# Stick-breaking attention: the sums over later key blocks as one running sum

## The chip, the cores and the metric

The kernel runs on one core of one Trainium2 chip. The metric is the device time of one execution in microseconds (us). Before the change three runs took 2278.54, 2282.21 and 2282.85 us; their median is 2282.21 us. All else is read from one profiled execution.

## The reference

The kernel computes a chain of layers for 512 positions of width 1024: a state-space layer with a feed-forward layer, a stick-breaking attention layer with a feed-forward layer, a softmax attention layer and a long-convolution layer. The change touches the stick-breaking attention alone. It has 16 heads of width 64, four query blocks and four key blocks of 128:

```python
z = jnp.einsum('bhqd,bhkd->bhqk', qb, kb).astype(jnp.float32)
...
causal = s_idx < t_idx
log_beta = jax.nn.log_sigmoid(z)
log_one_minus = jnp.where(causal, log_beta - z, 0.0)
rem = lax.cumsum(log_one_minus, axis=3, reverse=True) - log_one_minus
w = jnp.where(causal, jnp.exp(log_beta + rem), 0.0)
outs.append(jnp.einsum('bhqk,bhkd->bhqd', w.astype(vb.dtype), vb))
```

With sp(z) = log(1 + exp(z)) = -(log_beta - z), the exponent of a weight is z minus the sum of sp over the key itself and all later causal keys. So each key needs the sum of sp over the later keys of its own block, and over every later block.

## The kernel before, in words

Keys lie on the partitions and queries along the free dimension. `attn` (line 869) first makes the values V, then goes through eight pairs of heads, `b` = 0 to 7. For every second pair it loads and splits a weight tile for k and one for q (`weight`, line 169: the upper part `wh` on ScalarE, the remainder `wl` on VectorE, 128x256 at a time, line 185). For each pair it projects k and q (`proj`, 24 matmuls of 512 columns each), scales them into `kq`, and splits them into `kh`, `kl` and `qh`, `ql` (`ready`, `split`, line 159: the upper part by ScalarE, the remainder by VectorE). Then it calls `sb_heads` (line 940).

All matrix products run in fp32r on numbers split into an upper and a lower part. `sb_heads` works through a pair of heads in three units. Unit 0 holds key blocks 3 and 2 (256 queries each, 128x1024 for both heads; query columns before 256 are not causal for them), unit 1 key block 1 (384 queries, 128x768), unit 2 key block 0 (512 queries, 128x1024). Of each unit:

1. TensorE makes the scores z in a double PSUM tile `pair` (line 956), and adds the causal mask as a product (line 960). There are two such tiles, so unit 2 waits for unit 0's to be read.
2. VectorE takes |z| (line 964, "first step" below), ScalarE exp and ln(1 + .), VectorE adds max(z, 0) (line 967): `e` is the softplus sp. `e` has two buffers (`sbe`).
3. ScalarE rounds `e` to its upper part `sph`, VectorE subtracts for the remainder `spl` (lines 970 and 971; in the profile lines 152 and 140, the helpers).
4. TensorE adds the negative sums onto z (line 982): for the unit's own block with the triangular matrix `ntri`, and for every later block with a matrix of minus ones, `nones`, which sums a block's columns. For this the list `done` keeps the sph and spl of all units so far. A block is four matmuls: upper and lower part, two heads.
5. ScalarE takes exp of the whole unit from PSUM: the weights `wt` (line 985).

After unit 2 the weights times V go into `obank` (line 992), and `oraw` keeps the result. After pair 7 the upper and lower parts of `oraw` are the input of `attn_out`.

The order of the work on each engine is set when the program is built: a scheduler interleaves the projections of the next pair with the sums of the present one, and each engine then runs its list in order, waiting where an input is late. GpSimd has no instruction in the eight pairs.

Of the kernel before, what the change touches and what calls it, by code (L numbers as in the profile page):

```python
# [9 lines left out]
F32 = mybir.dt.float32  # L10
F32R = mybir.dt.float32r
# [3 lines left out]
ALU = mybir.AluOpType  # L15
# [3 lines left out]
P = 128  # L19
S = 512  # L20
# [30 lines left out]
class Kern:  # L51
# [817 lines left out]
    def attn(self):  # L869
        nc, a = self.nc, self.a  # L870
        xn = self.h
        wkv, wq = a["kv_w"], a["attn_w_q"][0]
        with self.sbuf("sb") as sp:
# [7 lines left out]
            mask = self.t([P, 3, P], BF16, "mask", 1, sp)  # L881
            self.act(mask, raw, AF.Copy)
            idr = self.t([P, P], BF16, "idr", 1, sp)
            self.act(idr, self.ident, AF.Copy)
            nones = self.t([P, P], F32R, "nones", 1, sp)
# [5 lines left out]
            self.act(ntri, traw, AF.Copy, scale=-1.0)  # L891

            V = sp.tile([P, 4, D], F32, name="V")
            pend = []
# [18 lines left out]
            os = []  # L913
            for b in range(KB):
# [5 lines left out]
                for n, wt, s in (("k", wk, 1.0), ("q", wqq, 0.125)):  # L920
# [4 lines left out]
                    kq += self.ready(t, None, self.hl(sp, n, 2))  # L925
                os.append(self.sb_heads(sp, b, *kq, V, mask, idr, nones, ntri))
            return [self.ready(o, None, self.hl(self.hp, "h", 8)) for o in os]
# [11 lines left out]

    def sb_heads(self, sp, b, kh, kl, qh, ql, V, mask, idr, nones, ntri):  # L940

# [3 lines left out]
        units = (((3, 256, 0), (2, 256, 256)), ((1, 128, 0),), ((0, 0, 0),))  # L945
        done, wts = [], {}
        for u, parts in enumerate(units):
# [19 lines left out]
            self.stt(e, zv, 0.0, e, ALU.max, ALU.add)  # L967
            sh = self.t([P, 2, W], F32R, f"sph{u}", 2 if u == 0 else 1, sp)
            sl = self.t([P, 2, W], F32R, f"spl{u}", 2 if u == 0 else 1, sp)
            self.act(sh, e, AF.Copy)  # L970
            self.tt(sl, e, sh.bitcast(F32), ALU.subtract)
            for p in parts:
                done.append(p + ((sh, sl),))
            for kb, q0, c0 in parts:
                for kk, qq, cc, sps in done:
                    if kk < kb:
                        continue
                    lhs = ntri if kk == kb else nones
                    for t in sps:
                        for h in range(2):  # L980
                            n = S - qq
                            mm(z[:, h, c0 + qq - q0 : c0 + S - q0], lhs, t[:, h, cc : cc + n],  # L982
                               start=False, stop=True, skip_group_check=True)
            wt = self.t([P, 2, W], F32, f"wt{u}", 1, sp)
# [1081 lines left out]
```

## Time and profile before

| what | value |
|---|---|
| median of three runs | 2282.21 us |
| profiled execution, its own time | 2278.72 us |
| its span, first to last instruction | 2277.0 us |
| mean granted TensorE clock | 0.953 |
| TensorE busy | 2111.4 us, 93% |
| VectorE busy | 1487.8 us, 65% |
| ScalarE busy | 987.9 us, 43% |
| GpSimd busy | 532.0 us, 23% |

Busy times are shares of the whole span; the eight head pairs take 839 to 1037 us of it. In the profile PE is TensorE, DVE VectorE, ACT ScalarE and POOL GpSimd. A line is often that of a helper: line 140 is any `tensor_tensor`, 143 any `scalar_tensor_tensor`, 147 and 149 any `tensor_scalar`, 152 any activation, 192 to 194 the three matmuls of a projection step. A row of the timeline with x2 merges two instructions that follow each other.

### The profile page before, as it was taken

The numbers are of one execution on the slowest core, as the hardware profiler recorded it, in microseconds if no ns is written. First come the engines' busy times: TensorE is split into PE (matmuls) and PEld (weight loads), VectorE is DVE, ScalarE is ACT, GpSimd is POOL, SyncE is SP. The second block draws the span as 40 slices with busy tenths as digits, with TensorE's granted clock in tenths as the row PEclk, the third lists the DMA queues.
The fourth block names the chain that finished last, engine by engine and source line by source line (L and its number), as shares of the span: only waits on it lengthen the run. The fifth ranks groups of instructions, "written<-read, shape, count | busy, mean of one in ns | idle before, by whom it ended". The sixth has DMA issues, their size and how long they took to land.

```text
span 2277.0 us, 29820 instructions
## 1 busy us (share of the span) xinstructions
PE 2111.4 (93%) x11732; PEld 1762.2 (77%) x11732; DVE 1487.8 (65%) x2348; ACT 987.9 (43%) x1496; POOL 532.0 (23%) x471
## 2 busy tenths in 40 slices
PE   6689999999999999989999999989999998888897
PEld 5478888788888887767778878888888877777776
DVE  9787864767665546664665675475687753988843
ACT  5555443332233446664442233434587653222232
POOL 4778621000000100001000000322243333324321
PEclk9789899999999999999999999989999998999899
DMA  5222163334432311112233552312000032222221
GB/s 163 69 62 77 64 206 98 125 99 138 157 125 77 109 59 60 50 38 65 93 120 125 160 177 83 102 52 69 27 1 1 20 111 74 77 91 84 65 74 56
DMA packets 194515, 199.36 MB, mean 88 GB/s; under 512 B 15059, under 2 KB 184550, under 8 KB 194311
## 3 DMA queue, kind: packets, MB, share of 16 engines
q1 hardware_dynamic: 179703, 183.11, 25.3%
q10 hardware_dynamic: 14672, 14.35, 2.1%
q8 instruction: 92, 1.51, 0.3%
q14 instruction: 48, 0.39, 0.1%
HBM read 182.75 MB, written 14.68 MB: 87 GB/s over the span
## 4 chain that ended last, share of the span: by engine, by line
PE 68%; DVE 17%; POOL 4%; issue 4%; ACT 4%; DMA 3%; SPq 0%; DVEq 0%; ACTq 0%; POOLq 0%
PE bank L192 16%; PE bank L194 15%; PE bank L193 15%; PE sc L1376 2%; PE pair L982 2%; DVE spt L140 2%; POOL tm L140 2%; DVE X L140 2%; DVE Y L140 2%; DVE wl L140 1%; PE obank L1799 1%; DMA adaraw<-in_ada_w_dram 1%; DMA wraw<-in_ffn_w_up_dram 1%; ACT wh L152 1%; PE sc L1517 1%
## 5 line engine op out<-in xcount | busy, mean ns | idle before, releaser
L192 PE MATMUL bank<-hh,wh 128*128 128x512 f32 x1472 | 592.9, 403 | 13.8 <-DVE v L143 7.5
L194 PE MATMUL bank<-hh,wl 128*128 128x512 f32 x1472 | 589.8, 401 | 13.3 <-DVE wl L140 13.3
L193 PE MATMUL bank<-hl,wh 128*128 128x512 f32 x1472 | 589.4, 400 | 0.5 <-DVE hl L143 0.5
L152 ACT ACTIVATE wh<-wraw 128x1024 fp32r<-128x1024 f32 (+2 forms) x260 | 245.3, 962 | 352.4 <-PE bank L193 195.2
L140 POOL TENSOR_TENSOR sqa<-sqa,sq 128x512 f32<-128x512 f32 x47 | 70.1, 1492 | 1180.6 <-ACT sq L152 1180.6
L194 PEld LDWEIGHTS bank<-hh,wl 128*128 128x128 f32 x1472 | 283.0, 192 | 78.5 <-DVE wl L140 18.0
L192 PEld LDWEIGHTS bank<-hh,wh 128*128 128x128 f32 x1472 | 282.3, 192 | 77.1 <-issue 7.5
L193 PEld LDWEIGHTS bank<-hl,wh 128*128 128x128 f32 x1472 | 282.6, 192 | 61.9 <-DVE hl L143 2.1
L140 DVE TENSOR_TENSOR wl<-wraw,wh 128x1024 fp32r<-128x1024 f32 (+2 forms) x220 | 245.6, 1133 | 109.3 <-ACT wh L152 108.7
L140 POOL TENSOR_TENSOR wl<-wraw,wh 128x1024 fp32r<-128x1024 f32 x40 | 102.8, 2588 | 177.9 <-ACT wh L152 177.8
L192 PE MATMUL bank<-ah,wh 128*128 128x512 f32 x352 | 137.8, 392 | 0.0
L193 PE MATMUL bank<-al,wh 128*128 128x512 f32 x352 | 137.0, 389 | 0.0
L194 PE MATMUL bank<-ah,wl 128*128 128x512 f32 x352 | 136.5, 390 | 0.3 <-DVE wl L140 0.2
L140 DVE TENSOR_TENSOR fg<-bank,rn 128x512 f32<-128x512 f32 x76 | 52.5, 690 | 106.1 <-PE bank L194 105.4
L140 POOL TENSOR_TENSOR sl<-sp,wh 128x768 fp32r<-128x768 f32 x32 | 59.4, 1857 | 107.8 <-ACT wh L152 57.4
L143 DVE SCALAR_TENSOR_TENSOR adaaccx<-adaraw,silc,adaaccx 128x256 f32<-128x256 f32 x168 | 81.0, 482 | 2.2
L194 PEld LDWEIGHTS bank<-ah,wl 128*128 128x128 f32 x352 | 66.1, 188 | 15.3 <-DVE wl L140 1.4
L193 PEld LDWEIGHTS bank<-al,wh 128*128 128x128 f32 x352 | 66.1, 188 | 13.5
L192 PEld LDWEIGHTS bank<-ah,wh 128*128 128x128 f32 x352 | 66.1, 188 | 13.3
L143 DVE SCALAR_TENSOR_TENSOR fy<-fg,prm,fy 128x511 f32<-128x511 f32 x88 | 65.9, 749 | 13.9 <-ACT fy L152 12.7
L140 POOL TENSOR_TENSOR fX<-spt 128x256 f32<-128x256 f32 x64 | 62.8, 1006 | 42.4 <-DVE spt L140 39.4
L1799 PE MATMUL obank<-X,idft 128*128 128x128 f32 x256 | 43.6, 326 | 29.2 <-DVE X L140 26.8
(557 smaller groups left out, 4328.9 us busy)
## 6 DMA issues: line engine op xcount, KB each, us to landing
wraw<-in_ffn_w_up_dram SPq DMA_DIRECT2D x88, 512.0 KB
adaraw<-in_ada_w_dram SPq DMA_DIRECT2D x24, 1024.0 KB
wraw<-in_ffn_w_down_dram SPq DMA_DIRECT2D x48, 384.0 KB
wraw<-in_hy_w_in_dram SPq DMA_DIRECT2D x32, 512.0 KB
wraw<-in_attn_w_in_dram SPq DMA_DIRECT2D x18, 512.0 KB
kspec<-fX SPq DMA_DIRECT2D x16, 512.0 KB
wraw<-in_ssm_w_glu_dram SPq DMA_DIRECT2D x16, 512.0 KB
wraw<-in_kv_w_dram SPq DMA_DIRECT2D x16, 512.0 KB
```

The lines of the kernel that those rows point to most:

```text
L140: (eng or self.nc.vector).tensor_tensor(out=out, in0=a, in1=b, op=op)
L143: self.nc.vector.scalar_tensor_tensor(out=out, in0=a, scalar=s, in1=b, op0=op0, op1=op1)
L152: return self.nc.scalar.activation(out, a, func, bias=bias, scale=scale, **k)
L192: mm(out, wh[k], xh, start=first and k == 0, stop=False)
L193: mm(out, wh[k], xl, start=False, stop=False)
L194: mm(out, wl[k], xh, start=False, stop=last and k == n - 1)
L982: mm(z[:, h, c0 + qq - q0 : c0 + S - q0], lhs, t[:, h, cc : cc + n], start=False, stop=True, skip_group_check=True)
L1376: mm(s, l, m[:, c], start=i == 0 and k % 2 == 0, stop=True, skip_group_check=True)
L1517: mm(s[:, k], ones, rows[u], start=False, stop=True, skip_group_check=True)
L1799: nc.tensor.matmul(ps[:, r * P : r * P + P], self.idft[:, j, r], Q[:, j, r], start=j == 0, stop=j == 1)
```

## The change

A tile `tail` (128 x 2 x 384, zero at the start) holds the sum of the softplus over the later key blocks. After unit 0, GpSimd adds the softplus of blocks 3 and 2 into its columns from 128 on; after unit 1, it adds `tail` onto unit 1's softplus, in place. Either sum is split into an upper part `sprh` (rounded by ScalarE) and a lower part `sprl` (subtracted by GpSimd). Units 1 and 2 then need one product of `nones` with this sum for all later blocks, where they had one for each. Inside unit 0 block 2 still sums block 3's own sph and spl. `sph` and `spl` of unit 0 have one buffer in place of two.

```diff
+            tail = self.t([P, 2, 384], F32, "tail", 1, sp)
+            nc.gpsimd.memset(tail, 0.0)
...
-        done, wts = [], {}
+        wts = {}
...
-            sh = self.t([P, 2, W], F32R, f"sph{u}", 2 if u == 0 else 1, sp)
-            sl = self.t([P, 2, W], F32R, f"spl{u}", 2 if u == 0 else 1, sp)
+            sh = self.t([P, 2, W], F32R, f"sph{u}", 1, sp)
+            sl = self.t([P, 2, W], F32R, f"spl{u}", 1, sp)
             self.act(sh, e, AF.Copy)
             self.tt(sl, e, sh.bitcast(F32), ALU.subtract)
-            for p in parts:
-                done.append(p + ((sh, sl),))
-            for kb, q0, c0 in parts:
-                for kk, qq, cc, sps in done:
-                    if kk < kb:
-                        continue
-                    lhs = ntri if kk == kb else nones
-                    for t in sps:
-                        for h in range(2):
-                            n = S - qq
-                            mm(z[:, h, c0 + qq - q0 : c0 + S - q0], lhs, t[:, h, cc : cc + n],
-                               start=False, stop=True, skip_group_check=True)
+
+            terms = [(q0, q0, c0, c0, (sh, sl), ntri) for _, q0, c0 in parts]
+            if u == 0:
+                terms.append((256, 256, 256, 0, (sh, sl), nones))
+            else:
+                (_, q0, c0), = parts
+                terms.append((q0, q0 + P, c0, q0, rest, nones))
+            for q0, qq, c0, cc, sps, lhs in terms:
+                for t in sps:
+                    for h in range(2):
+                        n = S - qq
+                        mm(z[:, h, c0 + qq - q0 : c0 + S - q0], lhs, t[:, h, cc : cc + n],
+                           start=False, stop=True, skip_group_check=True)
+
+            if u < 2:
+                rest = [self.t([P, 2, 384], F32R, f"spr{i}", 1, sp) for i in "hl"]
+                if u == 0:
+                    x = tail[:, :, P:]
+                    self.tt(x, e[:, :, :256], e[:, :, 256:], ALU.add, nc.gpsimd)
+                    hi, lo = (t[:, :, P:] for t in rest)
+                else:
+                    x = e
+                    self.tt(x, e, tail, ALU.add, nc.gpsimd)
+                    hi, lo = rest
+                self.split(x, hi, lo, nc.gpsimd)
```

The built order moves with it, in the eight pairs alone. Three places of pair 0 follow; the digit in a tile's name (sph0, spl1, wt2) is the unit.

TensorE, the sums of unit 2, before:

```order
L982 MATMUL pair_1164_7144<-sph0_1156_7094,nones_1105_6438 128x256 x2
L982 MATMUL pair_1164_7144<-spl0_1157_7095,nones_1105_6438 128x256 x2
L982 MATMUL pair_1164_7144<-sph0_1156_7094,nones_1105_6438 128x256 x2
L982 MATMUL pair_1164_7144<-spl0_1157_7095,nones_1105_6438 128x256 x2
L982 MATMUL pair_1164_7144<-sph1_1161_7126,nones_1105_6438 128x384 x2
L982 MATMUL pair_1164_7144<-spl1_1162_7127,nones_1105_6438 128x384 x2
L982 MATMUL pair_1164_7144<-sph2_1166_7158,ntri_1106_6440 128x512 x2
```

And now:

```order
L963 MATMUL pair_1184_7253<-mask_1103_6434,idr_1104_6436 128x384
L193 MATMUL bank_1213_7412<-hl_1093_6366,wh_1205_7368 128x512
L986 MATMUL pair_1169_7152<-spl2_1172_7167,ntri_1106_6440 128x512 x2
L986 MATMUL pair_1169_7152<-sprh_1166_7145,nones_1105_6438 128x384 x2
L986 MATMUL pair_1169_7152<-sprl_1167_7146,nones_1105_6438 128x384 x2
L194 MATMUL bank_1213_7412<-hh_1092_6365,wl_1206_7369 128x512
```

The six rows of column sums of units 0 and 1 have become two, of sprh and sprl, and these stand behind the unit's own spl2.

ScalarE, from unit 0's rounding on, before:

```order
L152 ACTIVATE sph0_1156_7094<-sbe_1155_7089 128x1024
L152 ACTIVATE sph1_1161_7126<-sbe_1160_7121 128x768
L152 ACTIVATE kh_1173_7218<-kq_1172_7216 128x512
L152 ACTIVATE wh_1196_7370<-wraw_1198_7372,prm1_882 128x256 x2
L152 ACTIVATE wh_1196_7370<-wraw_1199_7382,prm1_882 128x256 x3
L152 ACTIVATE wt0_1158_7110<-pair_1154_7074 128x1024
L152 ACTIVATE wh_1196_7370<-wraw_1199_7382,prm1_882 128x256
L152 ACTIVATE wt1_1163_7142<-pair_1159_7112 128x768
```

And now:

```order
L152 ACTIVATE sph0_1157_7096<-sbe_1156_7091 128x1024
L152 ACTIVATE sprh_1159_7112<-tail_1108_6444 128x2x256
L152 ACTIVATE sph1_1164_7133<-sbe_1163_7128 128x768
L152 ACTIVATE kh_1178_7218<-kq_1177_7216 128x512
L152 ACTIVATE wh_1205_7368<-wraw_1207_7370,prm1_882 128x256 x2
L152 ACTIVATE wh_1205_7368<-wraw_1208_7380,prm1_882 128x256 x2
L152 ACTIVATE wt0_1161_7117<-pair_1155_7076 128x1024
L152 ACTIVATE sprh_1166_7145<-sbe_1163_7128 128x768
L152 ACTIVATE wt1_1168_7150<-pair_1162_7119 128x768
```

A rounding of the first sum now stands ahead of sph1, and one of the second sum ahead of wt1, and so ahead of all that follows.

VectorE from unit 0's subtraction to unit 2's first step, before:

```order
L140 TENSOR_TENSOR spl0_1157_7095<-sbe_1155_7089,sph0_1156_7094 128x1024
L140 TENSOR_TENSOR spl1_1162_7127<-sbe_1160_7121,sph1_1161_7126 128x768
L140 TENSOR_TENSOR kl_1174_7219<-kq_1172_7216,kh_1173_7218 128x512
L143 SCALAR_TENSOR_TENSOR wl_1197_7371<-wraw_1198_7372,prm1_882,wh_1196_7370 128x256 x4
L143 SCALAR_TENSOR_TENSOR wl_1197_7371<-wraw_1199_7382,prm1_882,wh_1196_7370 128x256 x4
L147 TENSOR_SCALAR sbe_1165_7153<-pair_1164_7144 128x1024
```

And now:

```order
L140 TENSOR_TENSOR spl0_1158_7097<-sbe_1156_7091,sph0_1157_7096 128x1024
L140 TENSOR_TENSOR spl1_1165_7134<-sbe_1163_7128,sph1_1164_7133 128x768
L140 TENSOR_TENSOR kl_1179_7219<-kq_1177_7216,kh_1178_7218 128x512
L143 SCALAR_TENSOR_TENSOR wl_1206_7369<-wraw_1207_7370,prm1_882,wh_1205_7368 128x256 x4
L143 SCALAR_TENSOR_TENSOR wl_1206_7369<-wraw_1208_7380,prm1_882,wh_1205_7368 128x256 x2
L147 TENSOR_SCALAR sbe_1170_7161<-pair_1169_7152 128x1024
L143 SCALAR_TENSOR_TENSOR wl_1206_7369<-wraw_1208_7380,prm1_882,wh_1205_7368 128x256
```

Of the eight weight remainders ahead of the first step six are left, and the other two follow it.

GpSimd, its first instructions in the stage, where nothing stood before:

```order
L894 MEMSET tail_1108_6444 128x768
L140 TENSOR_TENSOR tail_1108_6444<-sbe_1156_7091 128x2x256
L140 TENSOR_TENSOR sprl_1160_7113<-tail_1108_6444,sprh_1159_7112 128x2x256
L140 TENSOR_TENSOR sbe_1163_7128<-sbe_1163_7128,tail_1108_6444 128x2x384
L140 TENSOR_TENSOR sprl_1167_7146<-sbe_1163_7128,sprh_1166_7145 128x768
```

Of these five the last four come back in each pair; in the program they stand between the rows of VectorE above.

## Rows read from the trace of the kernel before

**Rows 1.** Stretches: length, busy PE PEld DVE ACT POOL (count), granted clock, DMA, GB/s.

```profile
839.50:984.50 145.00, 144.02 (x814) 105.42 (x814) 92.95 (x126) 95.84 (x137) 0.00 (x0) 1.00 0.14 44
984.50:1036.60 52.10, 39.50 (x203) 28.42 (x199) 31.00 (x33) 32.39 (x39) 0.00 (x0) 0.84 0.13 41
```

**Rows 2.** List of waits, TensorE, 839 to 985 us: total us, times, longest us.

```profile
PE obank L992 <- ACT wt L152: 1.0, 3, 0.3
```

**Rows 3.** Timeline, TensorE: start us, us, engine, line, op, tile, shapes, count.

```profile
897.73 0.40 PE L982 MATMUL pair<-sph,nones 128*128 128x256 f32 x2
897.96 0.40 PE L982 MATMUL pair<-spl,nones 128*128 128x256 f32 x2
```

**Rows 4.** Chain that ended last, pair 0: start us, us, what.

```profile
853.40 0.29 PE bank L192
...
858.11 0.32 PE pair L956 x2
```

**Rows 5.** Line 140, GpSimd: count, ns min/median/max, first and last start us, forms.

```profile
L140 POOL TENSOR_TENSOR sqa<-sqa,sq x47: 1287/1420/1999, 331.7 to 2259.4; 128x512 f32<-128x512 f32 x47
L140 POOL TENSOR_TENSOR sl<-sp,wh x32: 1814/1833/2577, 1628.0 to 1839.7; 128x768 fp32r<-128x768 f32 x32
```

**Rows 6.** Timeline, GpSimd and VectorE, output projection.

```profile
1061.65 1.93 POOL L140 TENSOR_TENSOR sqa<-sqa,sq 128x512 f32<-128x512 f32 x1 [5.22 <-ACT sq L152]
...
1060.07 2.36 DVE L140 TENSOR_TENSOR wl<-wraw,wh 128x1024 fp32r<-128x1024 f32 x2 [0.17 <-ACT wh L152]
1062.35 1.78 DVE L143 SCALAR_TENSOR_TENSOR hl<-xT,prm,hh 128x512 fp32r<-128x512 f32 x1
```

**Rows 7.** Lines 140 and 143, VectorE, same columns as rows 5.

```profile
L140 DVE TENSOR_TENSOR ff<-bank,fdec x32: 657/692/693, 128.3 to 296.5; 128x512 f32<-128x512 f32 x32
...
L140 DVE TENSOR_TENSOR fab<-fab,fab x16: 676/807/1981, 131.2 to 297.9; 128x512 f32<-128x512 f32 x16
...
L143 DVE SCALAR_TENSOR_TENSOR hl<-xT,prm,hh x16: 748/1404/1791, 320.8 to 1084.7; 128x512 fp32r<-128x512 f32 x16
```

**Rows 8.** Timeline, VectorE, pair 0.

```profile
845.26 2.09 DVE L143 SCALAR_TENSOR_TENSOR sbe<-pair,sbe 128x1024 f32<-128x1024 f32 x2 [1.95 <-ACT sbe L152]
...
847.87 2.09 DVE L140 TENSOR_TENSOR spl<-sbe,sph 128x1024 fp32r<-128x1024 f32 x2
...
850.47 3.25 DVE L143 SCALAR_TENSOR_TENSOR wl<-wraw,prm,wh 128x256 fp32r<-128x256 f32 x8
853.63 1.22 DVE L147 TENSOR_SCALAR sbe<-pair 128x1024 int32<-128x1024 int32 x1
```

**Rows 9.** Timeline, ScalarE, pair 0.

```profile
846.67 1.78 ACT L152 ACTIVATE sph<-sbe 128x1024 fp32r<-128x1024 f32 x2
848.35 0.62 ACT L152 ACTIVATE kh<-kq 128x512 fp32r<-128x512 f32 x1
...
857.27 0.62 ACT L152 ACTIVATE qh<-kq 128x512 fp32r<-128x512 f32 x1
```

**Rows 10.** Timeline, VectorE, pair 3, unit 2: the first step.

```profile
924.51 1.22 DVE L147 TENSOR_SCALAR sbe<-pair 128x1024 int32<-128x1024 int32 x1 [1.57 <-PE pair L960]
```

**Rows 11.** Timeline, VectorE, pair 6, and the first step of pair 7.

```profile
991.78 2.09 DVE L140 TENSOR_TENSOR spl<-sbe,sph 128x1024 fp32r<-128x1024 f32 x2
...
996.90 1.22 DVE L140 TENSOR_TENSOR wl<-wraw,wh 128x1024 fp32r<-128x1024 f32 x1
998.03 1.22 DVE L147 TENSOR_SCALAR sbe<-pair 128x1024 int32<-128x1024 int32 x1
...
1004.97 1.22 DVE L140 TENSOR_TENSOR spl<-sbe,sph 128x1024 fp32r<-128x1024 f32 x1
...
1010.26 1.22 DVE L147 TENSOR_SCALAR sbe<-pair 128x1024 int32<-128x1024 int32 x1 [2.33 <-PE pair L960]
```

**Rows 12.** Stretches as in rows 1, two of 2 us in the second part.

```profile
1000.00:1002.00 2.00, 0.00 (x0) 0.00 (x0) 2.00 (x3) 1.97 (x4) 0.00 (x0) 0.93 0.50 177
1006.00:1008.00 2.00, 2.00 (x9) 1.35 (x9) 1.41 (x2) 0.68 (x1) 0.00 (x0) 0.50 0.79 266
```

More of the change, by code (lines that the diff above doesn't have):

```diff
@@ L925, in attn @@
                     kq += self.ready(t, None, self.hl(sp, n, 2))
-                os.append(self.sb_heads(sp, b, *kq, V, mask, idr, nones, ntri))
+                os.append(self.sb_heads(sp, b, *kq, V, mask, idr, nones, ntri, tail))
             return [self.ready(o, None, self.hl(self.hp, "h", 8)) for o in os]
@@ L938, in attn_out, with sb_heads @@
                 done(m)
-    def sb_heads(self, sp, b, kh, kl, qh, ql, V, mask, idr, nones, ntri):
+    def sb_heads(self, sp, b, kh, kl, qh, ql, V, mask, idr, nones, ntri, tail):
         nc = self.nc
```

## The prediction

> **What bounds the kernel now.** First the stage: the change lies in the attention of the second layer alone, and the table of stretches shows it as 839.5 to 1036.6 us, in two parts [rows 1]. In the first, 145 us, TensorE is busy 144.0 us at full clock while VectorE has 93.0 and ScalarE 95.8; the list of waits gives TensorE 1.0 us of idle time there [rows 2]. So any TensorE work that goes is time, unless something else becomes late. In the second, 52.1 us, the projections that fill TensorE's gaps run out: it is busy 39.5 us at a mean clock of 0.84, and the chain goes through VectorE and ScalarE. GpSimd does nothing in either. Behind the stage the output projection starts at once, so what the stage gains or loses reaches the end in full.
>
> Second, the pace of TensorE. Matmul durations overlap; the cost is the distance between starts. Four 256-column matmuls start in two rows 0.235 us apart: 0.118 us each [rows 3]. A 512-column projection matmul costs 0.235 us: 20 of them stand between the starts 853.40 and 858.11 [rows 4].
>
> **The change part by part.** *Removed.* Per head pair three blocks of column sums, each of four 256-column matmuls: 12, and 96 in eight pairs (320 matmuls of this line become 224). At 0.118 us that is 1.42 us a pair, 11.3 us in all; 8.5 us lie in the first part (pairs 0 to 5), and 2.8 us in the second, where they only count if nothing later takes their place.
>
> *Added on GpSimd.* Per pair an addition and a subtraction on 128x512, and the same on 128x768. The rows give 1.29 us (the least of 47 accumulations) and 1.83 us (the median of 32 subtractions) [rows 5], so 6.2 us a pair, 50 us in all. That is a quarter of the stage: GpSimd doesn't become the bound. The views of 2x256 occur nowhere before; I take the contiguous price, and the median of the accumulation, 1.42 us, as the upper one (0.3 us more a pair). The 128x768 memset of the tail stands ahead of the first pair's addition in a queue that is empty in the stage: nothing; uncovered it would cost less than a 128x768 operation with two inputs, 1.8 us.
>
> *Added on ScalarE.* Two roundings a pair: 0.62 us like kh for 512 columns, some 0.8 for 768 (sph0 and sph1 take 1.78 together) [rows 9]: 11.6 us in 197, onto 128 busy. It fits, but each stands in ScalarE's queue in front of other steps and waits there for GpSimd: the first in front of sph1, the second in front of wt1 and unit 2's exponential.
>
> *Single buffers.* sph0 and spl0 need one buffer, as only their own unit reads them. The two spr tiles are written again at the earliest 1.8 us (one GpSimd addition) after their last reader could start. Nothing.
>
> *What decides: GpSimd and VectorE in each other's way.* The trace has such pairs of operations [rows 6]. GpSimd's 128x512 addition at 1061.65 took 1.93 us, where 1.29 is its least: it waited until VectorE's two subtractions ended at about 1062.4. VectorE's remainder at 1062.35 then took 1.78 us, where 0.75 is its least [rows 7]: it waited until GpSimd was through. So they take turns, each for a whole instruction. Between 130 and 300 us, where GpSimd works most, the product of a PSUM and an SBUF tile (ff) never rose above 0.69 us, and the sum of two SBUF tiles of the same size (fab) reached 1.98 [rows 7]. I read it so: an instruction of VectorE with two SBUF inputs (spl, kl, ql, the weight remainders wl, hl) excludes a GpSimd operation, one that reads PSUM doesn't. The Trainium skill says the same as a rule that speaks against this change (SBUF — State Buffer, section "Who interferes with whom": a VectorE instruction with two SBUF inputs contends with a GpSimd instruction that reads SBUF, and whichever comes second is blocked entirely). By the rule the sum is the one that follows; without it, rival A. The rows bear the rule out.
>
> Now pair 0, by the rows of VectorE and ScalarE [rows 8, 9] and the new order. The first softplus is ready at 846.4. GpSimd adds 846.5 to 847.8 while VectorE reads PSUM. Rounding to 848.5; sph1 moves 0.7 us back, to 849.2. GpSimd's subtraction is due at 848.5, but VectorE is in spl0 until 849.1, so 849.1 to 850.4; spl1, which began at 849.0, now runs 850.4 to 851.4. kl follows to 852.0. GpSimd's second addition is due at 851.4, gets in behind kl, 852.0 to 853.8, and VectorE's weight remainders (0.4 us each) stand. While ScalarE rounds, three of them pass; GpSimd's second subtraction runs 855.0 to 856.8; the last three go to 858.0. Only then comes the first step of unit 2, at 853.63 before: **4.4 us late**. The next pair's qh, which follows it on ScalarE, ended at 857.9 and now ends at about 862.3. TensorE meanwhile: spl1 and the tail's sums to 852.2, three projections and unit 2's scores to 854.0, 20 projections to 858.7. There stands a matmul that needs qh: 3.6 us of waiting, and 0.6 more before sph2 and spl2, together 4.2.
>
> Pairs 2 and 4 have the weight remainders in other places; walked in the same way they wait 3.0 us (sph1 1.7, sph2 1.1, spl2 0.2) and 2.7 us (qh 1.9, sph2 0.8). Pairs 1, 3 and 5 have hardly any remainders, and VectorE is idle 1.6 us before unit 2's first step [rows 10], so GpSimd's second half costs nothing. What stays is spl1 behind the first subtraction (0.65 us) and the second rounding in front of the exponential (0.6): 1.25 each. First part: 4.2 + 3.0 + 2.7 + 3 x 1.25 = 13.7 us of waits against 8.5 removed, **+5.2 us**. The waits are late VectorE and ScalarE results; none can be filled, as each engine's order is fixed.
>
> Second part, pair 6 [rows 11]. spl1 ends at 995.2 in place of 993.9; kl; GpSimd's addition 995.8 to 997.6; two hl to 998.8; the subtraction 998.8 to 1000.7; then wl and hl, and unit 2's first step at 1002.4, which was at 998.03. spl2, with one more wl ahead on either engine, ends at about 1011.3 instead of 1006.1. Pair 7's first step began at 1010.26, 4.2 us after spl2; now there remain behind spl2 two 512-column and four 384-column matmuls at half clock (0.9 and 1.3 us) and 0.4 us of scores and masks, so it begins at about 1013.9, 3.6 us later. Pair 7 loses nothing more: its last sums end within 0.2 us of the old place, because spl2 ends them in both versions and the removed matmuls ran beside it. So **+3.6 us**.
>
> Sum: 5.2 + 3.6 = **+8.8 us**. The profiled execution took 2278.7 us (span 2277.0 and 1.7 around it); it would become 2287.5. The median of the runs is 2282.2, 3.5 above it, so I forecast 2282.2 + 8.8 = **2291.0 us**.
>
> **The rivals.** A change under 0.2% (4.6 us) can't be told from none here.
>
> A, faster: the two engines don't exclude each other on these operations, or meet at other moments. Then the walk leaves waits of 0, 0.5 and 0.7 us in the even pairs and 0.6 in the odd, 3.0 together, against 8.5; the second part keeps its time. -5.5 us: 2276.7; with no waits at all and all 96 matmuls gained, 2270.9. It decides where unit 2's first step of an even pair comes less than about 1 us late. For it: the projections in the new order stand as if nothing were late (20 before qh in both). Against it: the collisions [rows 6]. Chance 0.15.
>
> B, no difference: the collisions are real, but half of the 17.3 us of waits that I count falls beside projections or is lost by GpSimd and not by VectorE: 2282.2 + 8.8 - 8.7 = 2282.3. Chance 0.25, as I let VectorE lose every doubtful turn.
>
> C, worse: the waits make TensorE fall to the lower clock. After standing still from 1000 to 1002 it ran at 0.50, the 1.2 GHz level, and still did between 1006 and 1008 [rows 12]; 6 us at half pace cost 3 us of work. Once in each even pair: +9, 2300. Chance 0.10.
>
> That the work isn't removed is all but excluded by the order, in which the rows are gone; I keep 0.02 within B's case.
>
> **How the numbers follow.** My own case has 0.50, C 0.10: slower 0.60. B gives the same, 0.25; A faster, 0.15. The range runs from 2276 (A's time, without its full gain) to 2299 (most of C).
>
> **What would show it.** In the changed profile: 224 matmuls of column sums with unchanged pace; GpSimd busy some 50 us more in the stage, its subtractions longer than 1.3 and 1.8 us where VectorE runs spl or wl; wl and hl of VectorE stretched from 0.48 and 0.69 us to over 2; TensorE idle by 2 to 4 us near the end of pairs 0, 2 and 4, released by qh or sph; the last pair, from its first step to the stage's end, as long as before (26.3 us). If TensorE stays busy through the first part and the stage is 5 us or more shorter, the prediction is wrong, and the collisions don't carry over to these operations.

## The result, and the profile after

The changed kernel took 2295.24 us (median of 7 runs, 2290.35 to 2301.14); the kernel before, on the same chip, 2282.21 us (7 runs, 2277.34 to 2283.8). The ratio is 1.0064, 95% interval 1.005 to 1.0078: 13.0 us **slower**, where 8.8 were forecast.

The profiled execution of the changed kernel took 2301.14 us, the longest of its seven. So it stands 22.4 us above that of before, and not all of this is the change. The stage separates it. I measure the stage from the first step of pair 0 on VectorE to the first matmul of the output projection: 841.23 to 1036.60 us before, **195.4 us**, and 843.39 to 1051.51 after, **208.1 us**: 12.7 us longer, near the 13.0 us between the medians. The rest of the gap lies outside the stage (2.2 us ahead of it, 7.5 behind it).

The stage after, as stretches: pairs 0 to 5, pair 6, pair 7 to the output projection (columns as in [rows 1]).

```profile
843.39:990.14 146.75, 140.08 (x734) 98.70 (x735) 102.44 (x126) 103.54 (x150) 41.13 (x24) 0.97 0.14 44
990.14:1019.98 29.84, 21.29 (x98) 14.96 (x100) 24.46 (x24) 20.59 (x27) 7.07 (x4) 0.79 0.21 70
1019.98:1051.51 31.53, 19.73 (x77) 11.16 (x77) 11.07 (x10) 13.98 (x16) 6.98 (x4) 0.61 0.00 1
```

The same three of the kernel before, cut at the same events:

```profile
841.23:985.11 143.88, 142.90 (x805) 104.61 (x806) 92.95 (x127) 96.27 (x138) 0.00 (x0) 1.00 0.14 45
985.11:1010.26 25.15, 21.91 (x109) 16.62 (x109) 20.35 (x23) 19.16 (x25) 0.00 (x0) 0.86 0.23 77
1010.26:1036.60 26.34, 16.97 (x88) 11.57 (x88) 10.64 (x10) 12.81 (x15) 0.00 (x0) 0.81 0.02 8
```

So the loss is +2.9, +4.7 and +5.2 us. GpSimd works 55.2 us in the stage, and VectorE is busy 138.0 us in place of 123.9 with the same number of instructions. Read the third line: pair 7 has 11 matmul records fewer, and TensorE is busy 2.8 us longer, at a granted clock of 0.61 in place of 0.81.

What TensorE waits for now, pairs 0 to 5 (total us, times, longest us), where [rows 2] had 1.0 us:

```profile
PE pair L959 <- ACT qh L152: 4.5, 3, 3.2
PE pair L986 <- ACT sph L152: 1.5, 3, 0.8
PE obank L1008 <- ACT wt L152: 0.3, 1, 0.3
PE pair L986 <- DVE spl L140: 0.3, 1, 0.3
```

Pair 0 on GpSimd, then on VectorE (start us, us; where a row holds one instruction, x1). The place is that of [rows 8], with the stage starting 2.16 us later.

```profile
848.79 1.30 POOL L140 TENSOR_TENSOR tail<-sbe 128x512 f32<-128x512 f32 x1 [69.66 <-DVE sbe L143]
850.83 1.55 POOL L140 TENSOR_TENSOR sprl<-tail,sprh 128x512 fp32r<-128x512 f32 x1 [0.74 <-ACT sprh L152]
853.28 2.22 POOL L140 TENSOR_TENSOR sbe<-sbe,tail 128x768 f32<-128x768 f32 x1 [0.90 <-DVE spl L140]
856.46 1.85 POOL L140 TENSOR_TENSOR sprl<-sbe,sprh 128x768 fp32r<-128x768 f32 x1 [0.96 <-ACT sprh L152]
...
851.52 1.68 DVE L140 TENSOR_TENSOR spl<-sbe,sph 128x768 fp32r<-128x768 f32 x1 [0.29 <-ACT sph L152]
...
853.73 2.06 DVE L143 SCALAR_TENSOR_TENSOR wl<-wraw,prm,wh 128x256 fp32r<-128x256 f32 x1
...
853.73 5.66 DVE L143 SCALAR_TENSOR_TENSOR wl<-wraw,prm,wh 128x256 fp32r<-128x256 f32 x6
859.31 1.21 DVE L147 TENSOR_SCALAR sbe<-pair 128x1024 int32<-128x1024 int32 x1
```

The two engines take turns. The remainder of unit 1's softplus starts at 851.52 while GpSimd subtracts, and ends 0.8 us behind it, after 1.68 us where 0.95 is usual. The first weight remainder takes 2.06 us, to 0.3 us behind the end of GpSimd's addition. The six together take 5.66 us, where eight took 3.25 in [rows 8]. Unit 2's first step stands behind them. All remainders of this form, count and ns min/median/max:

```profile
L143 DVE SCALAR_TENSOR_TENSOR wl<-wraw,prm,wh x48: 466/475/2089, 853.7 to 966.5; 128x256 fp32r<-128x256 f32 x48
```

The median is that of before (0.48 us). Few are stretched, but one that is stands for what is left of GpSimd's operation.

### The profile page after: what moved, and what is told of

The parts are those of the page before. It is cut to its first block, busy times and chain, and to the rows that moved or that the text cites. A ratio compares the mean times of both kernels' runs of the same rounds, so it can differ in the third digit from the quotient of the medians.

```text
span 2299.4 us, 29704 instructions
## 1 busy us (share of the span) xinstructions
PE 2108.2 (92%) x11636; PEld 1749.1 (76%) x11636; DVE 1500.2 (65%) x2348; ACT 996.3 (43%) x1512; POOL 588.8 (26%) x504
## 4 chain that ended last, share of the span: by engine, by line
PE 40%; DVE 13%; ACT 3%; issue 3%; DMA 3%; POOL 1%; DVEq 0%; ACTq 0%; POOLq 0%
PE bank L194 8%; PE bank L192 8%; PE bank L193 8%; PE sc L1392 2%; DVE X L140 2%; DVE Y L140 2%; DVE spt L140 1%; PE pair L986 1%; PE obank L1815 1%; PE so L1553 1%; DVE wl L140 1%; PE sc L1533 1%; DMA wraw<-in_ffn_w_up_dram 1%; PE so L1556 1%; DMA adaraw<-in_ada_w_dram 1%
## 5 line engine op out<-in xcount | busy, mean ns | idle before, releaser
L192 PE MATMUL bank<-ah,wh 128*128 128x512 f32 x352 | 138.0, 392 | 1.3 <-ACT wh L152 1.3
L143 DVE SCALAR_TENSOR_TENSOR fy<-fg,prm,fy 128x511 f32<-128x511 f32 x88 | 65.9, 748 | 13.7 <-ACT fy L152 12.5
```

The lines of the kernel that those rows point to most:

```text
L143: self.nc.vector.scalar_tensor_tensor(out=out, in0=a, scalar=s, in1=b, op0=op0, op1=op1)
L192: mm(out, wh[k], xh, start=first and k == 0, stop=False)
```

## The experiments

One profiled execution outside the stage is between 2083 and 2100 us long for kernels that are equal there, so the stage is the sharper measure. It is read from one profiled execution of each run; the two kernels that were run twice repeat within 0.9 us (before and e9) and 0.1 us (e3 and e10), so a difference in the stage of less than 1 us shows nothing. In e1, e2, e5, e6 and e11 the later blocks are not all summed: they serve for their time alone. The table has, for every run, the whole time with its ratio to the runs of before on the same chip, the stage as defined above, and the distance from pair 0's first step to the first step of unit 2 in that pair.

| run | median us | ratio (95%) | stage us | unit 2 of pair 0, us |
|---|---|---|---|---|
| before | 2282.21 | | 195.4 | 12.40 |
| the change | 2295.24 | 1.0064 (1.005 to 1.0078) | 208.1 | 15.92 |
| e1 matmuls alone | 2277.12 | 0.9987 (0.9972 to 1.0003) | 185.3 | 12.42 |
| e2 nobody waits | 2293.75 | 1.0055 (1.0035 to 1.0075) | 204.4 | 15.92 |
| e3 on VectorE | 2278.71 | 0.9984 (0.9967 to 1.0001) | 184.4 | 13.17 |
| e4 two blocks | 2281.17 | 0.9999 (0.9979 to 1.0018) | 191.3 | 13.51 |
| e5 GpSimd alone | 2304.49 | 1.0095 (1.0075 to 1.0115) | 211.0 | 16.70 |
| e6 roundings alone | 2275.43 | 0.9978 (0.9962 to 0.9993) | 185.1 | 12.64 |
| e7 last pair's order | 2300.18 | 1.0076 (1.0057 to 1.0094) | 207.5 | 15.92 |
| e8 roundings later | 2302.63 | 1.0089 (1.0069 to 1.0109) | 208.3 | 15.54 |
| e9 before again | 2284.45 | 1.0023 (1.0007 to 1.0038) | 196.3 | 12.41 |
| e10 on VectorE again | 2275.24 | 0.9976 (0.9963 to 0.9989) | 184.3 | 13.17 |
| e11 GpSimd memsets | 2280.41 | 0.999 (0.9977 to 1.0003) | 187.0 | 12.39 |

**e1, the matmuls alone.** The tail product reads the tiles of the unit before, and the block that makes the running sum is gone.

```diff
-                terms.append((q0, q0 + P, c0, q0, rest, nones))
+                terms.append((q0, q0 + P, c0, 0, prev, nones))
...
-            if u < 2:
-                rest = [self.t([P, 2, 384], F32R, f"spr{i}", 1, sp) for i in "hl"]
...
-                self.split(x, hi, lo, nc.gpsimd)
+            prev = (sh, sl)
```

> The change's matmuls alone: the tail product of units 1 and 2 reads the hi and lo tiles of the unit before (same count and widths), and the running sum, its two roundings and GpSimd's four operations are left out (so the later blocks are not all summed). If the loss of the change comes from making the running sum (by taking turns with VectorE, or by a longer chain), this must be faster than before by most of the removed matmuls: 8.5 us of pairs 0 to 5 and up to 11.3 in all, 2271 to 2276 us. Rival: the removed matmuls were hidden or the scheduler's other order of the work is what costs; then 2280 or more, in the extreme the 2295 of the change.

The stage lost 10.1 us of the 11.3 that the 96 matmuls are worth. The whole time fell by 4.8 us, less than expected (2277.1 where 2271 to 2276 stood), with an interval that just reaches no change. By the stage, the matmuls were on the path and their price was right; the whole-time figure is less sharp (see e9).

**e2, nobody waits for the running sum.** The block stays, and the tiles of the unit before feed the tail product as in e1.

```diff
-                terms.append((q0, q0 + P, c0, q0, rest, nones))
+                terms.append((q0, q0 + P, c0, 0, prev, nones))
...
                 self.split(x, hi, lo, nc.gpsimd)
+            prev = (sh, sl)
```

> The change with all its GpSimd and ScalarE work, but the tail products read the hi and lo tiles of the unit before, so no matmul waits for the running sum (which nothing uses then). Theory of turns: GpSimd still shuts VectorE out and the roundings still stand in ScalarE's queue, so the loss stays, 2288 to 2296 us. Theory of the chain: what costs is that units 1 and 2 wait for the running sum; then the matmuls' gain shows, 2271 to 2278 us.

The whole time stays at 1.0055, the stage at 204.4 us, and pair 0's unit 2 is late by the same 3.5 us. So 9.0 of the 12.7 us are there although no matmul needs the sum. That the other 3.7 us are waiting for the sum is not shown: with the change itself TensorE's list of waits names neither `sprh` nor `sprl` anywhere in the stage, and the lists of e2 are ordered anew.

**e3, the four operations on VectorE.**

```diff
-                    self.tt(x, e[:, :, :256], e[:, :, 256:], ALU.add, nc.gpsimd)
+                    self.tt(x, e[:, :, :256], e[:, :, 256:], ALU.add)
...
-                    self.tt(x, e, tail, ALU.add, nc.gpsimd)
+                    self.tt(x, e, tail, ALU.add)
...
-                self.split(x, hi, lo, nc.gpsimd)
+                self.split(x, hi, lo)
```

> The change with the four GpSimd operations of a pair on VectorE: no two engines at one port, but VectorE has some 3.7 us more a pair (two of 0.75 us, two of about 1.1). Theory of turns: the stretched instructions go (VectorE's weight remainders back to 0.48 us), and the loss shrinks by more than half, to 2282 to 2288 us. Rival, the number of steps in VectorE's and ScalarE's queues ahead of unit 2 is what costs, whoever makes them: 2292 to 2297 us.

Better than either theory had it. The stage is 184.4 us, 11.0 shorter than before and 23.7 shorter than with the change, although VectorE takes on the four operations. These are the added ones, and the weight remainders (busy us, mean ns; the remainders: ns min/median/max), VectorE in e3:

```profile
L140 DVE TENSOR_TENSOR sbe<-sbe,tail 128x768 f32<-128x768 f32 x8 | 7.6, 952 | 0.1
L140 DVE TENSOR_TENSOR sprl<-sbe,sprh 128x768 fp32r<-128x768 f32 x8 | 7.6, 952 | 0.3 <-ACT sprh L152 0.2
...
L140 DVE TENSOR_TENSOR tail<-sbe 128x512 f32<-128x512 f32 x8 | 5.5, 686 | 0.1
L140 DVE TENSOR_TENSOR sprl<-tail,sprh 128x512 fp32r<-128x512 f32 x8 | 5.5, 685 | 0.0
...
L143 DVE SCALAR_TENSOR_TENSOR wl<-wraw,prm,wh x48: 473/478/485, 853.5 to 962.9; 128x256 fp32r<-128x256 f32 x48
```

An addition of 128x768 takes 0.95 us here and 2.00 on GpSimd, and no remainder is stretched. TensorE's granted clock stays at 1.00 from 840 to 960 us. The amount of VectorE's work is not what costs: it is busy 147.5 us in this stage, and 138.0 with the change. But the two differ in the order too. In pair 0 of e3 four remainders and no `kl` stand ahead of unit 2's first step, where the change has six and `kl`; so of the 2.75 us between 13.17 and 15.92 some 1.4 are order by the usual times of these three.

**e4, two blocks.** The running sum covers blocks 3 and 2; unit 2 sums block 1 by itself.

```diff
-                terms.append((q0, q0 + P, c0, q0, rest, nones))
+                if u == 2:
+                    terms.append((q0, P, c0, 0, prev, nones))
+                terms.append((q0, 256, c0, 0, rest, nones))
...
-            if u < 2:
...
+            if u == 0:
+                rest = [self.t([P, 2, 256], F32R, f"spr{i}", 1, sp) for i in "hl"]
+                self.tt(tail, e[:, :, :256], e[:, :, 256:], ALU.add, nc.gpsimd)
+                self.split(tail, *rest, nc.gpsimd)
+            prev = (sh, sl)
```

> Half of the change: the running sum covers key blocks 3 and 2 only (one addition and one subtraction of 512 columns on GpSimd and one rounding, all right behind unit 0); unit 2 sums block 1 by itself as before. 64 of the 96 matmuls stay away (7.5 us) and the operations of 768 columns, which held back unit 2, are gone. Theory of turns and of the chain alike: only spl1 is held up, by about 1 us in a pair; 2277 to 2282 us, the same or faster than before. Rival, any GpSimd work in this stage costs in proportion (2.6 of 6.2 us a pair): waits of about 10 us against 7.5 removed, 2284 to 2288 us.

No change in the whole time, 4.1 us less in the stage: 3.4 of the 7.5 us are given back. GpSimd's work is less than half of the change's (24.5 us of 55.2) and unit 2 of pair 0 is 1.1 us late in place of 3.5. The rival's proportional loss doesn't show.

**e5, GpSimd alone.** In e2 the roundings go, and the subtractions take what is there.

```diff
-                self.split(x, hi, lo, nc.gpsimd)
+                self.tt(lo, x, y, ALU.subtract, nc.gpsimd)
```

Here `y` is unit 0's first half, or `tail`.

> GpSimd's four operations a pair alone: no roundings of the running sum, the subtractions take operands that are there already, nothing reads the results, the tail products read the tiles of the unit before (so the later blocks are not all summed). Measure: the stage, from pair 0's first step on VectorE to the first output projection, which took 195.4 us before, 208.1 with the change, 204.4 where nobody waits for the running sum, 185.3 with the matmuls alone. Theory of turns (VectorE is shut out while GpSimd works): most of the 19 us between the matmuls alone and nobody waits stays, stage 197 to 205. Rival, the roundings that stand in ScalarE's queue and wait for GpSimd: the stage falls to 185 to 190.

211.0 us: more than the change itself and above what either theory had, without a single result that anyone reads. Without roundings between them the operations of GpSimd run back to back, and VectorE is stretched more: the weight remainders take 0.70 us in the mean, where e2 has 0.59 and before 0.48. They in e5 (busy us, mean ns), and then VectorE in pair 0 of e5 up to unit 2's first step:

```profile
L143 DVE SCALAR_TENSOR_TENSOR wl<-wraw,prm,wh 128x256 fp32r<-128x256 f32 x48 | 30.8, 697 | 1.9 <-ACT wh L152 1.9
...
850.69 3.19 DVE L140 TENSOR_TENSOR spl<-sbe,sph 128x1024 fp32r<-128x1024 f32 x2
853.80 0.68 DVE L140 TENSOR_TENSOR kl<-kq,kh 128x512 fp32r<-128x512 f32 x1
854.41 6.42 DVE L143 SCALAR_TENSOR_TENSOR wl<-wraw,prm,wh 128x256 fp32r<-128x256 f32 x8
860.75 1.22 DVE L147 TENSOR_SCALAR sbe<-pair 128x1024 int32<-128x1024 int32 x1
```

This is the list of the kernel before, instruction for instruction [rows 8], and its end comes 4.3 us later (16.70 against 12.40): 1.1 us lie in the two `spl` (3.19 for 2.09 us), 3.2 in the eight remainders (6.42 for 3.25). In this place neither another order nor a rounding of the sum is left as a rival.

**e6, the roundings alone.** In e2 GpSimd's operations go, and ScalarE rounds `e` itself.

```diff
-                    self.tt(x, e[:, :, :256], e[:, :, 256:], ALU.add, nc.gpsimd)
+                    self.act(hi[:, :, P:], e[:, :, :256], AF.Copy)
...
-                    self.tt(x, e, tail, ALU.add, nc.gpsimd)
+                    self.act(hi, e, AF.Copy)
...
-                self.split(x, hi, lo, nc.gpsimd)
```

> The other half: the two roundings a pair on ScalarE, of the softplus tiles, so that they wait for no GpSimd work; GpSimd does nothing, nothing reads the results, the tail products read the tiles of the unit before (the later blocks are not all summed). Theory of turns: 11.6 us more of ScalarE's time in a stage in which it has 50 us to spare: stage 185 to 190 us. Rival, ScalarE's queue is what makes the loss: 197 to 205.

185.1 us, as with the matmuls alone. The time of ScalarE's two roundings costs nothing that shows; here they wait for nothing, and what their waiting costs is left to e5 and e8. e5 and e6 together say: GpSimd's work is enough to make the loss, the roundings alone are not. The scheduler orders the engines' lists anew for every version, so the 19 us between e6 and e2 hold what the new order does too; how much of them are collisions alone is not shown outside e5's pair 0.

**e7, the last pair's order.** The exponential of unit 0's weights is issued behind `sph1`, in pair 7 alone.

```diff
             self.act(sh, e, AF.Copy)
+            if b == 7 and u == 1:
+                with self.ordered(("Activation",)):
+                    self.act(*late, AF.Exp)
...
-            self.act(wt, zv, AF.Exp)
...
+            if b == 7 and u == 0:
+                late = (wt, zv)
+            else:
+                self.act(wt, zv, AF.Exp)
```

> The change, with one thing moved in the last pair: ScalarE rounds unit 1's softplus ahead of unit 0's weights, as in the kernel before, and not behind them. Theory: the weights wait for TensorE's sums at the lower clock (2.0 us), and the rounding, ready at 1029.3, stood behind them until 1031.2; so the last pair ends 1.5 to 2 us earlier, stage 206 to 207 in place of 208.1. Rival: the last pair's loss comes from the two GpSimd operations of 768 columns and the lower clock, and the rounding's place is hidden: 208.

The stage is 0.6 us shorter, which the stage's own scatter (0.9 us) covers; the 1.5 to 2 us of the theory didn't come. The rounding did move up, but TensorE was late next. In e7, `sph1` on ScalarE, `spl1` and unit 2's first step on VectorE, the first of unit 2's scores on TensorE:

```profile
1032.24 0.84 ACT L152 ACTIVATE sph<-sbe 128x768 fp32r<-128x768 f32 x1 [1.02 <-DVE sbe L143]
...
1033.12 0.96 DVE L140 TENSOR_TENSOR spl<-sbe,sph 128x768 fp32r<-128x768 f32 x1 [0.91 <-ACT sph L152]
1038.90 1.23 DVE L147 TENSOR_SCALAR sbe<-pair 128x1024 int32<-128x1024 int32 x1 [4.82 <-PE pair L963]
...
1034.30 0.79 PE L959 MATMUL pair<-qh,kh 64*128 64x512 f32 x1 [0.16 <-ACT wt L152]
```

From `spl1`'s end to the first step pass 4.82 us, where the change has 3.35. The scores wait for unit 0's weights and start 187.9 us behind the stage's start, with the change 188.0: they gain nothing from the earlier rounding.

**e8, the roundings later.** The first rounding of the running sum is issued behind `sph1`, the second behind `wt1`, in every pair.

```diff
+            if u == 1:
+                with self.ordered(("Activation",)):
+                    self.split(*part, nc.gpsimd)
             self.tt(sl, e, sh.bitcast(F32), ALU.subtract)
...
+            if u == 1:
+                with self.ordered(("Activation",)):
+                    self.split(x, hi, lo, nc.gpsimd)
```

> The change, with the roundings of the running sum later in ScalarE's queue: the first behind unit 1's own rounding, the second behind unit 1's weights, so that ScalarE does not stand and wait for GpSimd. Theory of turns: VectorE is still shut out, but spl1 no longer stands behind the first subtraction; 1 to 4 us of the 12.7 come back, stage 204 to 207 us. Rival, ScalarE's waiting is the cause: at least 8 us come back, stage below 200.

A miss for both: 208.3 us, nothing comes back. GpSimd's operations move onto other instructions of VectorE (weight remainders 0.68 us in the mean in place of 0.59, `spl` of 128x1024 1.35 in place of 1.26). ScalarE's waits for GpSimd fall from 11.8 us in the stage to 3.6, and VectorE's busy time rises from 138.0 to 142.8, so e8 moves two things at once and doesn't clear ScalarE's waiting by itself. e5 shows that it isn't needed: there is no rounding of the sum in it, and it loses more.

**e9 and e10, once more.** The kernel before and e3, unchanged.

> The kernel before, run once more as an experiment, since the nine changed kernels spend 4 to 8 us more outside the attention stage than the one profiled execution of it. If that execution was only a short one, the stage is again 195 to 196 us, the rest 2086 to 2092 (it was 2083), and the ratio to itself 1.000. If the stage itself was short in it, the stage is 198 us or more, and all comparisons of the stage move by so much.

> The version with the four operations on VectorE once more, for its time against before: its stage was 11.0 us shorter, but its median only 3.3 us lower, with an interval that touched no change. If the stage's gain reaches the end, the two sessions together give 0.3 to 0.5% less than before (2272 to 2276 us); if something behind the stage takes it back, 0.1% or less.

The stage repeats within 1 us: 196.3 and 184.3. The whole time doesn't as well: the kernel before against itself gives 1.0023 with an interval that leaves out 1, and its profiled execution spent 2100 us outside the stage, not the 2086 to 2092 expected. So an interval here is too narrow by some 0.2%, and e3 and e10 (0.9984 and 0.9976) don't show by the whole time alone that they are faster. The 11 us of the stage are not seen in full in the whole time, nor are e1's and e6's 10. It is the same for the slower versions: median less stage, the kernel before is 2085 to 2088 us outside the stage (e9 with it), the change 2087, and the ten other runs 2089 to 2094, whichever way their stage went. What these 1 to 9 us are stays open.

**e11, memsets.** In place of GpSimd's operations, in e2 without the roundings:

```diff
+                for _ in range(2):
+                    nc.gpsimd.memset(x, 0.0)
+                    nc.gpsimd.memset(lo, 0.0)
```

> GpSimd busy, but reading nothing: in place of its four operations a pair, eight memsets into the same tiles, each started by the same softplus tiles once VectorE is through with them; no roundings, nothing reads the results, the tail products read the tiles of the unit before (the later blocks are not all summed). Theory of turns, in the form that two readers of SBUF shut each other out: VectorE's weight remainders keep their 0.48 us, and the stage is 184 to 188 us as with the matmuls alone. Rival, any GpSimd instruction shuts VectorE out: remainders stretched, and the stage 195 us or more, as with the four operations alone (211).

Of the memsets only the 32 that write the softplus tiles run in the stage; the others nothing held back, and they ran ahead of it. GpSimd and VectorE in e11 (busy us, mean ns; for the remainders ns min/median/max):

```profile
L992 POOL MEMSET sbe<- 128x768 f32 x16 | 11.8, 740 | 31.4 <-DVE spl L140 30.9
L992 POOL MEMSET sbe<- 128x512 f32 x16 | 8.4, 526 | 167.6 <-DVE spl L140 167.1
...
L143 DVE SCALAR_TENSOR_TENSOR wl<-wraw,prm,wh x48: 474/481/486, 852.1 to 956.3; 128x256 fp32r<-128x256 f32 x48
```

20 us of memsets stretch no remainder, and pair 0 runs as before (12.39 us). By the trace 22 of VectorE's instructions with two SBUF inputs, 12 of them remainders, ran beside a memset, and none took longer than usual. The stage is 187.0 us, 1.7 above e1's. It is a little less work than the 24.5 us of e4, but e4 has remainders of up to 1.5 us and unit 2 late. The Trainium skill (SBUF — State Buffer, "Who interferes with whom") says that a GpSimd instruction which only writes SBUF doesn't contend with a VectorE instruction of two SBUF inputs; e11 agrees.

## Why the prediction was right, and where it wasn't

The sign, the cause and the range hold; 13.0 us came where 8.8 were forecast. The sum is nearer than its terms, and that is luck. The cause is shown where the lists are equal (pair 0, e5 against before, with e11 as the counterpart); over the whole stage the runs don't part collisions, order and clock.

**Removed matmuls: right.** The stage of e1 and e3 is 10.1 and 11.0 us shorter, of 11.3 us priced. That also corrects rival A: without collisions I left 3.0 us of waits in the first part and gave the second part no gain, -5.5; the stage shows twice that.

**That the stage's loss "reaches the end in full": not shown.** For the change 12.7 and 13.0 us agree; in the experiments the difference of the whole times lies 3 to 9 us above that of the stages, e9 with it.

**GpSimd's time: a tenth too small.** 50 us were forecast, 55.2 came. The additions of 128x512 took 1.34 us in the mean, the subtractions of 128x768 1.85; the additions of 128x768 took 2.00 in place of 1.83, and the subtractions of 128x512 1.71 in place of 1.29 (its shortest 1.43), as several waited for a `spl`, a `kl` or a remainder.

**The turns: right, and the walk of pair 0 too.** Forecast was unit 2's first step 4.4 us late; it is 3.5 (15.92 against 12.40). The qh of the next pair was to end 4.4 us late and TensorE to wait 3.6 us for it; it ended 4.0 us late, and TensorE waited 3.2. VectorE loses one instruction to every GpSimd operation that it meets, as walked.

**Pairs 1 to 5: the waits were too many.** I had 13.7 us in the first part. The list of waits above gives 6.6, of which 3.2 in pair 0. Pairs 2 and 4 wait 1.2 and 0.8 us where 3.0 and 2.7 were walked, the odd pairs at most 0.7 where 1.25 was. Two steps failed. In pair 2 the remainders didn't meet as walked: unit 2's first step comes 12.5 us after the pair's first, and came 12.4 before. In pair 4 it is 2.7 us late, but TensorE waits 0.8: the projections that stand between took up the rest, as rival B had it.

**The clock: rival C came, once.** After the 3.2 us of waiting, TensorE's granted clock was 0.50, the 1.2 GHz level, from 864 to 874. Four stretches of 1 us at its two ends (columns as in [rows 1]):

```profile
863.00:864.00 1.00, 0.00 (x0) 0.00 (x0) 0.54 (x2) 1.00 (x3) 0.00 (x0) 0.91 0.87 176
864.00:865.00 1.00, 0.89 (x3) 0.66 (x4) 1.00 (x2) 1.00 (x4) 0.00 (x0) 0.50 0.78 269
873.00:874.00 1.00, 1.00 (x4) 0.91 (x3) 0.42 (x2) 0.50 (x1) 0.00 (x0) 0.50 0.00 0
874.00:875.00 1.00, 1.00 (x6) 0.52 (x7) 0.25 (x1) 1.00 (x2) 0.00 (x0) 0.97 0.47 145
```

9.9 us of work at half pace are 4.9 us lost, where I had priced 3 per pair. The waits of 0.3 to 0.8 us in the other pairs leave the clock at 1.00. So pairs 0 to 5 add up: 8.5 gained, 5.6 more waiting (6.6 against 1.0), 4.9 of clock: +2.0, measured +2.9; 0.9 us I can't place. The forecast of +5.2 had more waits and no clock.

**Pair 6: a little small, from two errors that offset each other.** Forecast +3.6, measured +4.7. Unit 2's first step is 3.7 us later, walked 4.4, and spl2 ends 4.3 us later, walked 5.2; the wait for qh grew from 2.5 to 7.3 us. Behind spl2 I took off 1.6 us for the removed matmuls, and 0.4 us came on: scores and mask took some 2.1 us there, where I had left 0.4, with the granted clock at 0.50 to the pair's end. Before it was 0.50 too, from 1002 to 1008, and rose then.

**Pair 7: the step that failed.** "Pair 7 loses nothing more" was +5.2 us. I had looked at unit 2's last sums, and neither at the way to unit 2's first step nor at the clock. Pair 7 on VectorE, ScalarE and TensorE, before:

```profile
1015.71 0.68 DVE L140 TENSOR_TENSOR hl<-oraw,hh 128x512 fp32r<-128x512 f32 x1
...
1019.41 1.01 ACT L152 ACTIVATE wt<-pair 128x1024 f32<-128x1024 f32 x1
...
1021.41 0.79 PE L956 MATMUL pair<-qh,kh 64*128 64x512 f32 x1
...
1023.91 1.23 DVE L147 TENSOR_SCALAR sbe<-pair 128x1024 int32<-128x1024 int32 x1 [3.42 <-PE pair L960]
...
1034.30 2.38 PE L992 MATMUL obank<-wt,V 128*64 128x512 f32 x16 [1.11 <-ACT wt L152]
```

With the change:

```profile
1019.98 1.22 DVE L147 TENSOR_SCALAR sbe<-pair 128x1024 int32<-128x1024 int32 x1 [2.85 <-PE pair L963]
...
1025.42 1.12 DVE L140 TENSOR_TENSOR hl<-oraw,hh 128x512 fp32r<-128x512 f32 x1
...
1030.27 1.02 ACT L152 ACTIVATE wt<-pair 128x1024 f32<-128x1024 f32 x1 [2.01 <-PE pair L986]
1031.19 0.83 ACT L152 ACTIVATE sph<-sbe 128x768 fp32r<-128x768 f32 x1
...
1031.35 0.80 PE L959 MATMUL pair<-qh,kh 64*128 64x512 f32 x2 [1.11 <-ACT wt L152]
...
1036.37 1.22 DVE L147 TENSOR_SCALAR sbe<-pair 128x1024 int32<-128x1024 int32 x1 [3.35 <-PE pair L963]
...
1047.05 4.53 PE L1008 MATMUL obank<-wt,V 128*64 128x512 f32 x16 [1.11 <-ACT wt L152]
1051.51 0.51 PE L192 MATMUL bank<-hh,wh 128*128 128x512 f32 x1
```

Unit 2's first step comes 16.4 us after pair 7's first (before: 13.65), 2.7 later. Of these, 0.4 are VectorE's `hl`, stretched beside a GpSimd addition (1.12 for 0.68 us). The other 2.3 lie between unit 0's `spl` and the first step. Unit 2's scores need the tile that `wt0` reads. Before, TensorE made unit 1's sums over the later blocks while `wt0` ran, and began the scores at 1021.41, 1.0 us after its end; half of those sums are gone and the others stand behind the scores, so it now stands still for 1.1 us until `wt0` ends. And its granted clock is 0.50 from 1028 on, where before it was 0.50 from 1019 to 1022 and about 0.9 or more on either side. So the removed matmuls had covered a wait. That order stood in the lists before any run. Neither the rounding of the sum nor `sph1`, which stands behind `wt0`, is on this path: e7 moves `sph1` up, and the scores start where they did. Behind the first step 0.3 us more pass to the 16 output matmuls, and from these to the stage's end 2.2 us more (4.46 for 2.30): the granted clock was 0.50 from 1044 to 1048 us and 0.56 in the next 4 us, where before it was 0.94 from 1032 to 1036. That clock is not a matter of GpSimd alone: the same 16 take 2.38 us in e2, and 3.80 in e1, which has no GpSimd work.

The single buffer of `sprh`, put at nothing, held one rounding for 3.7 us in this pair, until TensorE had read the tile; it was not on the path either.

So of the three numbers 5.2, 3.6 and 0, measured were 2.9, 4.7 and 5.2. Rival B's part (waits hidden by projections) and C's (the clock) both came, and in the sum partly cancelled: 2.3 us too many in the first part, 6.3 too few in the second.

**What the changed profile was to show.** The matmuls, GpSimd's time and the stretched remainders (up to 2.09 us) came as listed, and so did pair 0's idle TensorE. Of GpSimd's subtractions those of 128x512 were longer as listed (1.43 to 2.33 us), those of 128x768 not (1.81 to 1.87). The 2 to 4 us of idle time in pairs 2 and 4 and the unchanged last pair didn't come.

**A version whose stage is shorter than both.** The same running sum made by VectorE (e3, e10) keeps the matmuls' gain: stage 184.4 and 184.3 us against 195.4 and 196.3. The whole time, 0.9984 and 0.9976, doesn't show the gain over the kernel before clear of e9's shift. Over the change it is clear: the slowest of its 22 runs, 2285.94 us, is below the fastest of the change, 2290.35.

## What to carry to other kernels

GpSimd was idle in this stage by the profile, and its work was still not free. So before work goes to it, look at which VectorE instructions with two SBUF inputs stand beside it, and charge each meeting with the rest of GpSimd's operation. VectorE's own price for the work (here about half of GpSimd's) may be the cheaper one even where VectorE is busy two thirds of the time. And walk the last pair of a stage as carefully as the first, on the order of the lists after the change: ask which wait the removed work had covered, and which clock TensorE will have there.

## What the runs showed that was not expected

- A GpSimd operation that VectorE met cost one VectorE instruction the rest of its time (2.06 and 2.09 us for remainders of 0.475), and the others passed between at their usual time. So the stretched ones are few and long, which a mean (589 ns) hides. GpSimd running back to back (e5, 211.0 us) lost more than with pauses (e2, 204.4), though the lists differ too.
- VectorE had room for the same work: 23.6 us more of it in e3 cost nothing that shows, 14.0 us of stretching came with a stage 12.7 us longer. Why the one hides and the other doesn't stays open; in pair 0 about half of the difference is order.
- 3.2 us without a matmul were followed by 9.9 us of work at the lower clock, 4.9 us lost; the waits of 0.3 to 0.8 us in pairs 1 to 5 were followed by none.
- The kernel before, run once more as a kernel of its own, differed from itself by 0.23% (0.07 to 0.38), while its stage agreed within 1 us. Such differences come from the other stages: profiled executions of before spend 2083 and 2100 us there.
